# TensorE's queue in the order of the program, with the program's steps traced in another order

## The chip, the cores and the metric

The kernel runs on one core of one Trainium2 chip. The metric is the device time of one execution in microseconds (us). TensorE is called PE here, VectorE DVE, ScalarE ACT, GpSimd POOL and SyncE SP.

## What is computed

Two blocks in sequence on 256 tokens of width 1024, in float32. The first block (`first_block`, called b1 in the kernel) has two layers: banded attention with a sink and a dilated mixture, and latent attention with a rotary key. The second block has two layers on the same tokens (x) and on 256 context tokens (ctx). Each layer is a mixer and an expert feed-forward, `peer_ffn`:

```python
p = xn @ wl                        # q, k, v, pool, conv, gates: 10 x 1024 columns
o = blocked_diff_attn(q, k, v, lam)
mix = mixer_output(o, p, ...)      # gated sum of attention, pooling and convolution, then @ w_out
h = h + mod[:, 2] * mix
# peer_ffn: 8 heads, the best 16 of 16384 experts each
q = (xc @ w_q).reshape(chunk, 8, 2, 128)
s = einsum('thid,hikd->thik', q, sub_keys)        # two half keys, top 16 of each
# top 16 of the 256 sums, softmax -> gate, expert indices eidx
hid = gelu(einsum('td,thkd->thk', xc, u_emb[eidx]))
out = einsum('thk,thkd->td', gate * hid, v_emb[eidx])
```

The first layer's mixer runs on x and on ctx, the second's on x with only keys and values of ctx.

## The kernel before

**Work.** Activations lie transposed, channels on partitions, as eight chunks of 128 channels by 256 tokens. A weight chunk (128x1024 float32, 512 KB) makes 128 output channels of one product. Most chunks are split in two rounded halves `wa` (ACT, L281) and `wb` (DVE, L282), and multiply in 24 matmuls (L409 to L411, `mm3`). Chunks called whole skip the split and multiply as float32 (L416, `mm1`). `WS.get` loads three chunks ahead (two in the expert phase) and splits two ahead (one there).

**Experts.** `topk` makes the scores (L1241), picks the best 16 on DVE and transposes the choice (`id4`, L1344). `gbuild` turns the choice into a dense table of gates G (one-hot tables `hot` and `gat` on DVE, L1487 and L1489, matmuls L1495, ACT copies L1499, stores from the ACT queue L1504). `peer` then runs over all 128 expert rows: `hid(j)` multiplies chunk j of `pu` with x and applies gelu (L1528), `wgt(j)` multiplies with the gates `gp` (a load of G, L1548), `vside(j)` adds the product with chunk j of `pv` (L1570 to L1580). The first `npre` of the `hid` run before G is there, into buffers `gpre`; the first `nnat` of `pu` are whole. In layer 0 the experts of ctx are instead gathered row by row (`rows`: indirect loads from the POOL queue L1381, and on DVE L1392 and L1401), 512 row steps spread over other stages.

**Order.** The program is a set of Python generators that trace instructions; `par`, `lead`, `along` and `chain` decide by the numbers that are yielded (`yield 2.6`: a cost) which generator traces next. The context is opened with `schedule_with_timeline_sim=True`: a planner then sets each engine's queue by its own model of time. Of the instructions that are ready in that model it takes the one traced first, so that a later traced instruction comes ahead of one that waits there. On the chip each queue runs in the order so set. The planner also hands out the buffers: 42 of 4 KB a partition (tag `pg`, weight chunks and most activations), and PSUM banks, three of tag `u` for products and five of tag `m`.

**Stages.** b1 (`x`) runs beside the ctx mixer, its `choose` (the expert choice of ctx) and the modulation products (`mods`, L574): `lead(xs, (ctx..., 2.0))` gives ctx two units of cost for one of x. When ctx has come to its `rows`, x goes on alone with its own mixer (layer 0): `qkv`, then `attend` (`attn2`) and `branches` by `par` with rates 60 and 190. Then `ffn_start` (`topk`; then the rest of `topk`, `gbuild` and the early `hid` by `par`) and the loop of `peer`. Layer 1 follows in the same manner; there `kv_ctx` (the rest of the rows, the norm of ctx and its keys) and `attend` run beside `branches`.

**Norms.** `rms_bcast` squares on ACT (L472), sums on PE (L474, L479), makes the root on DVE (`rsqrt`, L403), a diagonal `dg` (L498), and spreads it with PE (L501). `norm_hl` and `norm_f` multiply and split. The head norm in `qkv` and the one after the attention have the same form (L946, L903, L905; L1046, L1056). The attentions run in three steps for each unit u: `first` (scores on PE, softmax on DVE and ACT), `second` (transposes, L656 and L1015), `third` (product with the values, L668 and L1026).

Of the kernel before, what the change touches and what calls it, by code (L numbers as in the profile page):

```python
# [34 lines left out]
NPRE = (16, 20), (20, 28)  # L35
# [257 lines left out]
class Ker:  # L293
# [170 lines left out]
    def rms_bcast(s, hch, n):  # L464

        nc = s.nc
        st = s.ps("m")
        if n == 8:

            for g in range(0, n, 4):  # L470
                sq = s.pg([128, 4, T], F32, "sq")
                nc.scalar.activation(sq, hch(g, 4), AF.Square)  # L472
                for k in range(4):
                    nc.tensor.matmul(st[32 * k:32 * k + 32, :T], s.ones[:, 0:32], sq[:, k], start=g == 0, stop=g == 4)  # L474
            gs = s.s1([128, T], "gs")
            nc.scalar.copy(gs, st[:, :T])
            ss = s.ps("m")
# [4 lines left out]
        else:  # L482
            for g in range(0, n, 4):
                m = min(4, n - g)
                sq = s.pg([128, 4, T], F32, "sq")
                nc.scalar.activation(sq[:, :m], hch(g, m), AF.Square)
                for k in range(m):
# [16 lines left out]
    def rms(s, h, n=8):  # L504
        rbs = s.s1([128, T], "rbs")
        s.nc.vector.tensor_copy(rbs, s.rms_bcast(lambda g, m: h.t[g // 4][:, :], n))
        return rbs

    def norm_hl(s, h, a, b, name, n=8, rbs=None):

        nc = s.nc
        rbs = rbs if rbs is not None else s.rms(h, n)
        o = HL(s, name, n)
        for k in range(n):
# [6 lines left out]
            else:  # L521
                nc.scalar.activation(oh, y, AF.Identity, bias=b(k))
                nc.vector.scalar_tensor_tensor(ol, y, b(k), oh, op0=OP.add, op1=OP.subtract)
        return o

    def norm_f(s, h, a, b, o):

        nc = s.nc
        rbs = s.rms(h)
        for k in range(8):  # L530
            y = s.s1([128, T], "ny")
            nc.vector.scalar_tensor_tensor(y, h.ch(k), a(k), rbs, op0=OP.mult, op1=OP.mult)
            nc.scalar.activation(o.ch(k), y, AF.Identity, bias=b(k))  # L533
        return o
# [88 lines left out]
    def attn_causal(s, scores, bias, init, scale, val, emit):  # L623
# [49 lines left out]
        for i in range(18):  # L673
            if i < 16:
                first(i)
            if 1 <= i < 17:
                second(i - 1)
            if i >= 2 and i % 2 == 1:
                third((i - 3) // 2)
            yield 1.7  # L680
# [12 lines left out]
    def b1(s, x, eng, out):  # L693
# [8 lines left out]
        hn = s.norm_hl(x, lambda k: s.V("norm_w", k), None, "hn")  # L702
        del x
        ws.load(W1)
        yield 1.0
# [81 lines left out]
        hn = s.norm_hl(x, lambda k: s.V("norm_w", 8 + k), None, "hn")  # L787
# [48 lines left out]
        cqn = s.norm_hl(cq, lambda k: s.V("cqn", k), None, "cqn", 2)  # L836
        ckn = s.norm_hl(ckv, lambda k: s.V("ckvn", k), None, "ckn", 1)
# [49 lines left out]
        rb = s.rms_bcast(lambda g, m: x.t[g // 4][:, :], 8)  # L887
# [7 lines left out]
    def rows_hl(s, rr, lo, n):  # L895
# [12 lines left out]
        nc.vector.tensor_tensor(rl[z], tb[z, :T], rh[z], op=OP.subtract)  # L908
        return rh[z], rl[z]


    def qkv(s, l, hn, ws, rope, want_q, r):
# [26 lines left out]
        for a, off, _ in todo:  # L939
            for hf in range(2):  # L940
                sq = s.pg([128, 4, T], F32, "sq")
                nc.scalar.activation(sq, a.t[hf], AF.Square)
                for k in range(4):
# [9 lines left out]
        rh, rl = s.rows_hl(rr, 0, 16)  # L953
        yield 8.0
# [29 lines left out]
    def attn2(s, l, q, kv, sr, o):  # L984
# [45 lines left out]
        for i in range(18):  # L1030
            if i < 16:
                first(i)
            if 1 <= i < 17:
                second(i - 1)
            if i >= 2:
                third(i - 2)
            yield 3.0

        bank = s.ps("m")
        for hf in range(2):  # L1040
            sq = s.pg([128, 4, T], F32, "sq")
            nc.scalar.activation(sq, o.t[hf], AF.Square)
            for k in range(4):
# [6 lines left out]
        rh, rl = s.rows_hl(rr, 64, 8)  # L1050
        yield 4.0
# [108 lines left out]
    def mixer(s, l, st, src, ws, eng, res, kvx, late=None, before=None, seq=False, h=None, rbs=None, side=None):  # L1160
# [7 lines left out]
        hn = s.norm_hl(h, lambda k: s.a1[l][:, k, st:st + 1], m0, "hn", rbs=rbs)  # L1168
# [50 lines left out]
        res["xn"] = s.norm_f(h, lambda k: s.a2[l][:, k, st:st + 1], s.mod(l, st, 3), Act(s, F32, "xn"))  # L1219
# [3 lines left out]
    def topk(s, l, xn, ws, eng, res, rows=False):  # L1223
# [8 lines left out]
        for h, sb in s.lin(ws, xn, 16):  # L1232
            if sb is None:
                yield 2.6
                continue
            qf = s.s2([128, 512], "qf")
            nc.scalar.copy(qf, sb)
# [17 lines left out]
            if h % 4 < 3:  # L1255
                continue
# [38 lines left out]
            for j in range(2):  # L1295
                for hf in range(2):
# [13 lines left out]
                    yield TY  # L1310
        ts = tp[:, 2].rearrange("p h t k -> p (h t) k")
# [158 lines left out]
    def gbuild(s, res, G, eng, ntc=8):  # L1470
# [7 lines left out]
        iob = io[:, None, :, :].to_broadcast(sh)  # L1478
        for tc in range(ntc):
            gt = [s.pg([128, 32, 32], F32, "gt") for _ in range(4)]  # L1480
            for q in range(4):
# [8 lines left out]
                for u in range(2):  # L1490
# [277 lines left out]
```

## Time and profile before

| | before |
|---|---|
| runs | 3692.51 to 3705.2 us, median of 3: 3701.63 us |
| profiled execution, own time | 3691.09 us |
| its span (first to last instruction) | 3689.3 us |
| PE busy | 3258.1 us, 88% |
| DVE busy | 2790.7 us, 76% |
| ACT busy | 1485.0 us, 40% |
| mean granted clock of PE | 0.932 of full |
| DMA | 941.10 MB, mean 255 GB/s |

Busy time is the union of an engine's instructions. A row with an idle time names what ended it. The granted clock has two levels, 1.2 and 2.4 GHz (0.5 and 1.0 in the rows); a mean between them says how the stretch divides.

### The profile page before, as it was taken

How to read it: one execution, taken by the hardware profiler on the slowest of the kernel's cores; microseconds unless marked ns; L12 is line 12 of the kernel's file. 1: busy time of each engine (PE TensorE's matmuls, PEld its weight loads, DVE VectorE, ACT ScalarE, POOL GpSimd, SP SyncE). 2: the span in 40 equal slices, each digit the busy share in tenths (PEclk: the TensorE clock that was granted, in tenths of full speed). 3: DMA queues.
4: the chain of work that ended last, by engine and by line, in shares of the span. 5: the costliest groups of instructions: out<-in, count | busy, mean ns of one | idle time of the engine just before them, and what ended most of it. 6: DMA issues, size and time to landing. Idle time of an engine off the chain costs nothing. (4 is left out here: it accounts for less than half of the span.)

```text
span 3689.3 us, 61049 instructions
## 1 busy us (share of the span) xinstructions
PE 3258.1 (88%) x23324; PEld 2966.9 (80%) x23324; DVE 2790.7 (76%) x5722; ACT 1485.0 (40%) x2785; POOL 935.6 (25%) x831
## 2 busy tenths in 40 slices
PE   6989989996799885679999999778998689999999
PEld 5976889766689774668888888767988589999999
DVE  4356585578899889799989999788465978777655
ACT  3444345323355313333443444333353154444443
POOL 2002101212343512365555555232000003111000
PEclk9989999998899897889999999888999899999999
DMA  8536446756688845999999999776525089888764
GB/s 298 160 126 215 146 138 189 274 183 225 238 299 280 321 161 181 344 408 386 384 379 386 379 387 381 248 280 231 158 88 192 12 262 354 307 285 286 263 217 153
DMA packets 315430, 941.10 MB, mean 255 GB/s; under 512 B 29616, under 2 KB 93136, under 8 KB 315136
## 3 DMA queue, kind: packets, MB, share of 16 engines
q1 hardware_dynamic: 130848, 468.77, 35.7%
q0 software_dynamic: 118816, 432.76, 32.3%
q10 hardware_dynamic: 65472, 35.66, 3.2%
q8 instruction: 183, 3.00, 0.3%
q14 instruction: 111, 0.91, 0.1%
HBM read 893.01 MB, written 43.02 MB: 254 GB/s over the span
## 5 line engine op out<-in xcount | busy, mean ns | idle before, releaser
L282 DVE TENSOR_TENSOR wb<-wr,wa 128x1024 fp32r<-128x1024 f32 x846 | 1015.4, 1222 | 321.5 <-ACT wa L281 304.9
L281 ACT CAST wa<-wr 128x1024 fp32r<-128x1024 f32 x846 | 856.3, 1046 | 108.3 <-DMA wr<-in_w 39.0
L409 PE MATMUL pu<-hnh,wa 128*128 128x256 f32 x2000 | 586.0, 293 | 47.9 <-ACT wa L281 45.9
L411 PE MATMUL pu<-hnh,wb 128*128 128x256 f32 x2000 | 583.4, 293 | 17.1 <-DVE wb L282 17.0
L410 PE MATMUL pu<-hnl,wa 128*128 128x256 f32 x2000 | 578.5, 290 | 0.0
L409 PE MATMUL pu<-xh,wa 128*128 128x256 f32 (+1 forms) x1760 | 492.1, 280 | 10.1 <-ACT wa L281 9.6
L1381 POOL DMA_INDIRECT row<-in_pu,ridx x256 | 365.1, 1426 | 520.7 <-DVE wb L282 124.5
L410 PE MATMUL pu<-xl,wa 128*128 128x256 f32 (+1 forms) x1760 | 491.2, 279 | 0.9 <-DVE xl L1538 0.9
L411 PE MATMUL pu<-xh,wb 128*128 128x256 f32 (+1 forms) x1760 | 491.4, 279 | 0.0
L1381 POOL DMA_INDIRECT row<-in_pv,ridx x256 | 354.4, 1384 | 473.5 <-DVE wb L282 133.0
L409 PEld LDWEIGHTS pu<-hnh,wa 128*128 128x128 f32 x2000 | 397.7, 199 | 65.0 <-ACT wa L281 52.0
L411 PEld LDWEIGHTS pu<-hnh,wb 128*128 128x128 f32 x2000 | 395.8, 198 | 32.5 <-DVE wb L282 21.9
L410 PEld LDWEIGHTS pu<-hnl,wa 128*128 128x128 f32 x2000 | 397.4, 199 | 3.9 <-issue 3.5
L409 PEld LDWEIGHTS pu<-xh,wa 128*128 128x128 f32 x1760 | 338.5, 192 | 20.1 <-ACT wa L281 14.5
L410 PEld LDWEIGHTS pu<-xl,wa 128*128 128x128 f32 x1760 | 338.5, 192 | 4.6 <-DVE xl L1538 1.1
L411 PEld LDWEIGHTS pu<-xh,wb 128*128 128x128 f32 x1760 | 338.5, 192 | 1.8 <-issue 0.4
L1401 DVE SCALAR_TENSOR_TENSOR racc<-row,rwg,racc 128x1024 f32<-128x1024 f32 x254 | 325.5, 1282 | 0.4
L416 PE MATMUL pu<-xn,wr 128*128 128x256 f32 (+1 forms) x1344 | 311.9, 389 | 4.7 <-ACT xn L533 4.7
L1392 DVE CUSTOM_DVE_ANT_0 row<-row,xr 128x1024 f32<-128x1024 f32 x256 | 311.2, 1221 | 0.0
L1528 ACT ACTIVATE gel<-pu 128x256 f32<-128x256 f32 (+1 forms) x208 | 77.2, 371 | 577.8 <-PE pu L411 553.0
L416 PEld LDWEIGHTS pu<-xn,wr 128*128 128x128 f32 x1344 | 261.6, 199 | 41.7 <-issue 6.2
L1570 PE MATMUL pm<-W,wa 128*128 128x224 f32 x1024 | 276.1, 275 | 1.6 <-ACT wa L281 1.6
(427 smaller groups left out, 6487.7 us busy)
## 6 DMA issues: line engine op xcount, KB each, us to landing
wr<-in_w SPq DMA_DIRECT2D x288, 512.0 KB
wr<-in_pu SPq DMA_DIRECT2D x256, 512.0 KB
wr<-in_pv SPq DMA_DIRECT2D x256, 512.0 KB
wr<-in_w POOLq DMA_DIRECT2D x130, 512.0 KB
wm<-in_wmod POOLq DMA_DIRECT2D x96, 512.0 KB
G<-gt ACTq DMA_DIRECT2D x60, 512.0 KB
gp<-G SPq DMA_DIRECT2D x32, 512.0 KB
gp<-G SPq DMA_DIRECT2D x32, 448.0 KB
```

The costliest lines, as they stand in the source:

```text
L281: nc.scalar.copy(a, r)
L282: nc.vector.tensor_tensor(b, r, a, op=OP.subtract)
L409: mm(out, ah, bh, start=i == 0, stop=False)
L410: mm(out, ah, bl, start=False, stop=False)
L411: mm(out, al, bh, start=False, stop=i == n - 1)
L416: s.nc.tensor.matmul(out, w[:, k * 128:(k + 1) * 128], x(k), start=k == 0, stop=k == 7)
L1381: nc.gpsimd.indirect_dma_start(out=t, out_offset=None, in_=tab[w], in_offset=bass.IndirectOffsetOnAxis(ap=s.ridx[:, tt, i:i + 1], axis=0))
L1392: v.tensor_tensor_reduce(t, t, xr[tt], 1.0, 0.0, OP.mult, OP.add, hid[:, i:i + 1])
L1401: v.scalar_tensor_tensor(out[tt], t, wg[:, i:i + 1], out[tt], op0=OP.mult, op1=OP.add)
L1528: nc.scalar.activation(g, bank[:, :NT], AF.Gelu_apprx_tanh)
L1570: mm(o, vh[:, c], W[:, 0], start=j == 0 and d % 2 == 0, stop=False, skip_group_check=True)
```

## The change

PE's queue is no longer the planner's: `manual_schedule` for PE makes it the order in which the program traces. The other engines and the buffers stay with the planner. With that the program traces in another order:

- `rms_bcast` yields between its steps, and with it `rms`, `norm_hl` and `norm_f`, which become generators; `rows_hl` and the head norms yield too. The context norm at the start is traced beside b1's.
- both attentions run `second` two steps behind `first` instead of one, `third` three or more behind, in 19 rounds instead of 18, of costs that keep the sum.
- `topk` traces the choice of a head (`select`) after the product of the next; `gbuild` traces the matmuls of a table (`tables`) after the one-hot tables of the next.
- `ffn_start` traces the early `hid` beside the tail of `topk` (`lead`, at 6 units for each unit of `topk` in layer 0, 4 in layer 1), and the rest beside `gbuild`, instead of all beside tail and `gbuild` by `par`.
- layer 0 takes `nnat, npre` = 20, 24 for 16, 20. Layer 1 keeps 20, 28.

```diff
-NPRE = (16, 20), (20, 28)
+NPRE = (20, 24), (20, 28)
+
+EARLY = (6.0, 50.0), (4.0, 65.0)
...
                 nc.scalar.activation(sq, hch(g, 4), AF.Square)
+                yield 1.5
                 for k in range(4):
                     nc.tensor.matmul(st[32 * k:32 * k + 32, :T], s.ones[:, 0:32], sq[:, k], start=g == 0, stop=g == 4)
             gs = s.s1([128, T], "gs")
             nc.scalar.copy(gs, st[:, :T])
+            yield 1.0
...
             nc.vector.tensor_scalar(dg[:, tt], s.C("ident"), r[:, tt:tt + 1], None, op0=OP.mult)
+        yield 4.0
         rb = s.ps("m")
...
-        for i in range(18):
+        for i in range(19):
             if i < 16:
                 first(i)
-            if 1 <= i < 17:
-                second(i - 1)
-            if i >= 2:
-                third(i - 2)
-            yield 3.0
+            if 2 <= i < 18:
+                second(i - 2)
+            if i >= 3:
+                third(i - 3)
+            yield 2.85
...
-        rh, rl = s.rows_hl(rr, 64, 8)
-        yield 4.0
+        yield 3.0
+        rh, rl = yield from s.rows_hl(rr, 64, 8)
...
+        prev = None
+        for h, sb in s.lin(ws, xn, 16):
+            if sb is None:
+                yield 2.6
+                continue
+            qf = s.s2([128, 512], "qf")
+            nc.scalar.copy(qf, sb)
+            if prev is not None:
+                yield from select(*prev)
+            prev = h, qf
+        yield 2.6
+        yield from select(*prev)
...
-        program(k, upto)
+
+        with tc.manual_schedule(engines={mybir.EngineType.PE}):
+            program(k, upto)
...
-def ffn_start(k, l, rx, ws, G, pe, tot, *more, ntc=8):
+def ffn_start(k, l, rx, ws, G, pe, early, tot, *more, ntc=8):
...
-    yield from par(k, (chain(tk, lambda: k.gbuild(rx, G, k.nc.scalar, ntc)), TG), (until(pe), tot), *more)
+    pre = until(pe)
+    yield from lead(tk, (pre, early))
+    yield from par(k, (k.gbuild(rx, G, k.nc.scalar, ntc), 64.0), (pre, tot), *more)
...
-    next(b1)
-    rbc = [k.rms(hc[0])]
     md = k.mods(0, gp)
+    rbc = []
+
+    def norm_ctx():
+        rbc.append((yield from k.rms(hc[0])))
+    drain(par(k, (until(b1), 1.0), (norm_ctx(), 1.0)))
     drain(until(md))
```

## Rows read from the trace of the kernel before

**Rows 1.** Page: busy us (share) of the engines; DVE's split, count, busy, mean ns.

```profile
PE 3258.1 (88%) x23324; PEld 2966.9 (80%) x23324; DVE 2790.7 (76%) x5722; ACT 1485.0 (40%) x2785; POOL 935.6 (25%) x831
...
L282 DVE TENSOR_TENSOR wb<-wr,wa 128x1024 fp32r<-128x1024 f32 x846 | 1015.4, 1222 | 321.5 <-ACT wa L281 304.9
```

**Rows 2.** Table by stretch; columns in its first line, x counts instructions.

```profile
core 0: us, PE busy (x) PEld busy (x) DVE busy (x) ACT busy (x) POOL busy (x), PEclk, DMA share, GB/s
190.00:300.00 110.00, 96.14 (x549) 78.37 (x549) 66.47 (x228) 49.97 (x149) 8.45 (x16) 0.78 0.37 120
440.00:540.00 100.00, 85.49 (x643) 82.72 (x643) 72.83 (x153) 39.06 (x58) 8.48 (x16) 0.90 0.37 120
840.00:1000.00 160.00, 117.95 (x753) 106.47 (x754) 128.13 (x261) 56.34 (x77) 47.14 (x37) 0.79 0.72 253
1000.00:1250.00 250.00, 234.43 (x1815) 221.50 (x1813) 233.70 (x399) 121.10 (x200) 102.56 (x73) 0.98 0.85 295
1370.00:1413.00 43.00, 2.06 (x9) 1.26 (x8) 40.96 (x227) 4.00 (x13) 0.94 (x1) 0.50 0.08 22
1413.00:1531.00 118.00, 91.75 (x719) 78.11 (x719) 109.30 (x167) 51.34 (x265) 35.38 (x26) 0.86 0.89 292
1700.00:2300.00 600.00, 556.78 (x3462) 499.85 (x3461) 549.25 (x725) 251.23 (x391) 328.92 (x223) 0.99 0.99 384
2350.00:2570.00 220.00, 176.03 (x1218) 165.53 (x1216) 180.75 (x285) 80.21 (x107) 64.64 (x55) 0.85 0.74 261
2914.00:2949.00 35.00, 5.67 (x27) 4.71 (x26) 33.26 (x184) 5.08 (x15) 0.00 (x0) 0.58 0.00 0
2949.00:3070.00 121.00, 109.25 (x984) 103.75 (x983) 83.81 (x127) 61.52 (x266) 7.46 (x7) 0.95 0.86 277
3100.00:3600.00 500.00, 500.00 (x4480) 500.00 (x4479) 358.71 (x471) 245.75 (x378) 65.97 (x51) 1.00 0.83 279
```

**Rows 3.** Timeline of PE, the norm of ctx in layer 1: start, us, instruction, [idle before].

```profile
2554.93 1.22 PE L501 MATMUL pm<-dg,ones 128*128 128x128 f32 x4 [2.74 <-DVE dg L498]
2563.03 0.58 PE L409 MATMUL pu<-hnch,wa 128*128 128x256 f32 x1 [6.87 <-ACT wa L281]
```

**Rows 4.** Timeline of PE, end of ctx's attention and start of b1's.

```profile
262.46 1.22 PE L757 MATMUL pm<-kava,q 64*128 64x256 f32 x2
...
266.17 0.87 PE L656 MATMUL pm<-ct,p 128*128 128x128 f32 x3 [2.07 <-DVE p L649]
266.84 6.82 PE L1046 MATMUL pm<-ones,sq 128*128 128x1 f32 x32
276.22 1.02 PE L903 MATMUL pm<-ct,rr 128*8 128x128 f32 x4 [2.56 <-DVE rr L403]
```

**Rows 5.** Timeline of PE, early `hid` chunk beside the table.

```profile
1434.38 3.67 PE L416 MATMUL pu<-xn,wr 128*128 128x256 f32 x16
```

**Rows 6.** Groups on DVE, 1413 to 1531: count | busy us, mean ns | idle before.

```profile
L1489 DVE TENSOR_TENSOR gat<-hot,id 128x1024 f16<-128x1024 f16 x64 | 41.4, 688 | 1.5
```

**Rows 7.** Waits of the SP queue from 1290 to 1560: us in total, times, longest.

```profile
SPq L268 <- DVE top L1309: 43.8, 1, 43.8
```

**Rows 8.** Timelines of ACT, SP and PE between the table and the expert loops.

```profile
1533.00 10.08 ACTq L1504 DMA_DIRECT2D G<-gt  x3
...
1543.29 0.33 SPq L1548 DMA_DIRECT2D gp<-G  x1
...
1560.91 1.71 PE L1578 MATMUL pm<-wa,W 128*128 128x512 f32 x4 [2.01 <-ACT wa L281]
...
3070.44 0.37 PE L1570 MATMUL pm<-W,wa 128*128 128x224 f32 x1 [1.38 <-ACT wa L281]
```

**Rows 9.** Timeline of PE, layer 0's attention norm: x16 squares, then a product.

```profile
1222.04 2.11 PE L1046 MATMUL pm<-ones,sq 128*128 128x1 f32 x16
1224.01 0.56 PE L409 MATMUL pu<-hnh,wa 128*128 128x256 f32 x1
```

**Rows 10.** Timeline of PE at the start.

```profile
52.27 0.58 PE L409 MATMUL pu<-hnh,wa 128*128 128x256 f32 x1 [6.08 <-ACT wa L281]
```

More of the change, by code (lines that the diff above doesn't have):

```diff
@@ L511, in norm_hl @@
         nc = s.nc
-        rbs = rbs if rbs is not None else s.rms(h, n)
+        if rbs is None:
+            rbs = yield from s.rms(h, n)
         o = HL(s, name, n)
@@ L528, in norm_f @@
         nc = s.nc
-        rbs = s.rms(h)
+        rbs = yield from s.rms(h)
         for k in range(8):
@@ L786, in b1 @@
         s.dump("x1", x)
-        hn = s.norm_hl(x, lambda k: s.V("norm_w", 8 + k), None, "hn")
+        hn = yield from s.norm_hl(x, lambda k: s.V("norm_w", 8 + k), None, "hn")
         yield 1.0
@@ L886, in b1 @@
         s.dump("x2", x)
-        rb = s.rms_bcast(lambda g, m: x.t[g // 4][:, :], 8)
+        rb = yield from s.rms_bcast(lambda g, m: x.t[g // 4][:, :], 8)
         for k in range(8):
@@ L1167, in mixer @@
         m0 = s.mod(l, st, 0)
[L1168 removed]
+        hn = yield from s.norm_hl(h, lambda k: s.a1[l][:, k, st:st + 1], m0, "hn", rbs=rbs)
         del h, rbs
@@ L1231, in topk, with select @@
         IX = s.sml([128, 8, 4, 16], "topi", H16, bufs=1)
[L1232 to L1237, printed above, removed]
+        def select(h, qf):
             sb = s.ps("m")
@@ L1478, in gbuild, with tables @@
         iob = io[:, None, :, :].to_broadcast(sh)
+        def tables(hot, gat, gt, tc, q):
+            for u in range(2):
+                bank = s.ps("m")
+                for i in range(4):
+                    t = u * 4 + i
+                    for j in range(2):
+                        mm(bank[:, i * 128:(i + 1) * 128], hot[:, 0, t // 2, :, t % 2], gat[:, j, t // 2, :, t % 2],
+                           start=j == 0, stop=j == 1)
+                for jq in range(4):
+                    o = q * 8 + u * 4
+                    nc.scalar.activation(gt[jq][:, :, o:o + 4],
+                                         bank.rearrange("p (t j) -> p j t", t=4)[:, jq * 32:(jq + 1) * 32, :],
+                                         AF.Copy, scale=1.0 / GS)
+                yield 1.0
+            if q < 3:
+                return
+            for jq in range(4):
+                eng.dma_start(G[jq * 8:(jq + 1) * 8, :, tc].rearrange("g p j t -> p g (j t)"),
+                              gt[jq].rearrange("p (g j) t -> p g (j t)", g=8))
+        prev = None
         for tc in range(ntc):
@@ L1489, in gbuild @@
                     v.tensor_tensor(gat[:, j], hot[:, 1], w[2 + j], op=OP.mult)
-                for u in range(2):
-                    bank = s.ps("m")
-                    for i in range(4):
-                        t = u * 4 + i
-                        for j in range(2):
-                            mm(bank[:, i * 128:(i + 1) * 128], hot[:, 0, t // 2, :, t % 2], gat[:, j, t // 2, :, t % 2],
-                               start=j == 0, stop=j == 1)
-                    for jq in range(4):
-                        o = q * 8 + u * 4
-                        nc.scalar.activation(gt[jq][:, :, o:o + 4],
-                                             bank.rearrange("p (t j) -> p j t", t=4)[:, jq * 32:(jq + 1) * 32, :],
-                                             AF.Copy, scale=1.0 / GS)
-                    yield 1.0
-            for jq in range(4):
-                eng.dma_start(G[jq * 8:(jq + 1) * 8, :, tc].rearrange("g p j t -> p g (j t)"),
-                              gt[jq].rearrange("p (g j) t -> p g (j t)", g=8))
+                if prev is not None:
+                    yield from tables(*prev)
+                prev = hot, gat, gt, tc, q
+        yield from tables(*prev)
     def peer(s, l, xn, G, eng, eng2, nnat, npre, out, keep=None, NT=T, rows=None):
```

44 lines of the change are left out of this document (26 added, 18 removed).

## The prediction

> **What bounds the kernel now.** I read the page first, then the table by stretch, then PE's timeline around its waits. PE is busy 88% of the span, more than any other engine [rows 1]. The table's clock column falls wherever PE is not dense [rows 2]. In it three kinds of stretch are to be told apart. From 3100 to 3600 PE is busy throughout at full clock: an order that only moves work can give nothing there. From 1700 to 2300 the DMA engines are busy 0.99 of the time, DVE 549 of 600 us and PE 557: three limits together. Everywhere else PE stands idle for some us at a time, waiting for a short chain on DVE and ACT, at half clock around it. These last are what the change is about.
>
> What such a stretch of length L loses I count as its idle time, plus half of that part of its low-clock time in which PE works. With mean clock m the low-clock time is 2(1-m)L, so the loss is idle + (2(1-m)L - idle)/2 where that is positive. By [rows 2], in us: 190 to 300 loses 13.9 + 17.2 = 31; 440 to 540 14.5 + 2.8 = 17; 840 to 1000 42 + 12.6 = 55; 1000 to 1250 16; 1370 to 1413 41; 1413 to 1531 26 + 3 = 30; 2350 to 2570 44 + 11 = 55; 2914 to 2949 29; 2949 to 3070 12. Of 286 us I have to say which part the new order reaches.
>
> The clock term is where the Trainium skill speaks against me. Its page "TensorE: Matmul & The Clock Gate", Part 1, says that for modelling the ramp costs under 1% of a typical span. By that rule all low clock here would cost under 37 us. The trace says otherwise: between 190 and 300 PE works 96 us at a mean clock of 0.78 [rows 2], and 17 us go there alone. The measurement decides; without the clock terms the sum below would be some 12 us smaller.
>
> **The change part by part.**
>
> *Norms with cover.* A norm is four PE steps with ACT and DVE between. With the yields, a product of the other generator now stands between them in PE's queue, where there is another generator: b1's second norm and its two small ones (ctx's `conv` to `co` chunks between, stretch 440 to 540), and ctx's norm in layer 1 (`branches` between). The first stretch loses 17; I take 13 (8 to 17, since the wait for the last split of the normed value remains). For the second the two waits are 2.74 and 6.87 us [rows 3]: 9.6, I take 10 with the clock around (0 to 20). No cover exists for the norm that ends b1, the first and second norm and the head norm of the x mixers: when they come, ctx is at its `rows` and no other generator traces PE work. So 840 to 1000, the largest loss, I set at 0 (-10 to 15). Norms: 23 (-2 to 52).
>
> *Attentions two steps apart.* Between 250 and 295 ctx's attention runs out of b1's products, which the planner had drawn ahead. Scores at 262.46, transposes of the unit before at 266.17 after 2.07 us idle, then the norm after the attention waits 2.56 more [rows 4]. In traced order b1's `z` chunks stay between the steps for two thirds of ctx's 16 units; after that its last units meet b1's own attention, as now. Of 31 I take half, 16 (0 to 25). In the x mixer of layer 0 each step has some 10 us of `branches` beside it either way; of 16 I take 8 (0 to 13). In layer 1 the attention's last units again outlast `branches`: 0. Attentions: 24 (0 to 38).
>
> *The start of the experts.* PE waits out the tail of `topk`: 41 us in layer 0, 29 in layer 1 [rows 2], for DVE. `lead` at 6 units a yield and 3.41 a chunk traces nine `hid` before the transposes of the choice; in layer 1, at 4 and 2.99, seven, and two just after. Nine chunks of 3.67 us [rows 5] are 33 us: they fit into 41. Each also issues its `pu` load on SP's queue; DMA share there is 0.08 in layer 0 and 0.00 in layer 1, so the loads cost nothing, if a buffer is free.
>
> What is late next? In layer 0 the table is DVE's: 64 `gat` of 688 ns [rows 6] and as many `hot`, 88 us, the rest of its 109 in 118 us [rows 2] being mostly row steps. It doesn't shrink when PE has less to do. After it ACT sits 10.08 us on the last stores of G, the first load of G issues at 1543.29, and `vside` starts at 1560.91 [rows 8]. That path remains, but nine 512 KB loads, 4.7 MB or 16 us at the 292 GB/s of this stretch, are no longer in its way. I take 10 (0 to 20). Four more `hid` before the loop take four loads out of it: 0.52 MB at 384 GB/s, 1.4 us each, 5 together. In exchange four chunks become whole and spare DVE's split. Layer 0: 15 (0 to 25).
>
> In layer 1 PE itself is the limit: busy 109 of 121 us [rows 2] until `vside` at 3070.44 [rows 8]. Nine chunks leave, 29 us. Then DVE's table (56 `hot`, 56 `gat`: 77 us from 2949) and the path through G are next: table until 3026, then the 28 us from the last stores to `vside` in layer 0 (1533.0 to 1560.9 [rows 8]) would allow 3054. So I take 16 (4 to 29). Start of the experts: 31 (4 to 54).
>
> *`topk` and `gbuild` a step later.* PE now has its next product ahead of the scores. The chain is DVE's in both; I take 0.
>
> *What the planner's order had hidden.* In front of traced order stands no later work. After layer 0's attention the squares at 1222.04 are followed at once by products of the gate after it [rows 9], which the program traces behind the whole norm. Without them PE waits for the evacuation of the last unit, the squares, the root and the spread: 2.56 us for the root where it stood open [rows 4], I take 7 in all, and the same in layer 1: -14 (-30 to -6). At the start b1's first products, now ahead of the modulation products, will queue behind these. PE stands idle 6.08 us before 52.27 for a later chunk's cast [rows 10], which covers most of that; -2 (-5 to 0). Sum -16 (-35 to -6).
>
> *Rows.* The new yields pace `rows` anew, on POOL's queue and DVE. In `ffn_start` the yields fall from 187 to 167, at 0.25 five row steps fewer; those that b1 and the x mixer gain (58 units, doubled for ctx, over 6.25) let some 15 more pass before. So ten fewer remain for layer 1. The steps move, none is added: 0.
>
> **Sum.** 23 + 24 + 31 - 16 = 62 us; all low ends -33, all high ends 138. The profiled execution took 3691.1 us; 62 less is 3629. The median of the runs shown lies 10.5 higher, and gives 3640. The middle of the ends, 52, lies close to the sum, but the places set at 0 hold the largest losses (840 to 1000), so I lean to the lower of the two and state 3632; the forecast's own range, some half of the way to the ends, is 40 us to either side: 3592 to 3672.
>
> **Rivals.**
>
> *Buffers hold the loads.* In layer 0 SP's `pu` load waited 43.8 us, to the end of DVE's choice, for a buffer [rows 7]. If early `hid` meet the same, nothing goes into the tail: 31 becomes 5, attentions reach half: 62 - 26 - 12 = 24, from the median 3677. For it: `tables` and `npre` 24 hold more buffers. Against: traced earlier, the loads come first when buffers are handed out, and each `hid` frees one.
>
> *More is reached than I count.* Half of what 840 to 1000 and the rest of 2350 to 2570 lose (55 + 45) and some of 1700 to 2300: 60 us on top of the forecast, 3572. By the Trainium skill's "Perfetto Trace Analysis", section Roofline, the 16 DMA engines give some 435 GB/s; then the loop of layer 0 would not be at its limit. Here the DMA engines are busy 0.99 at 384 GB/s [rows 2], so the measured limit is lower.
>
> *Slower: the queue stands at each attention step.* In traced order nothing passes a `second` whose softmax is late. From 190 to 300 PE works 96 us [rows 2] on some 22 units (ctx's 16, about six of b1) with the products between: 4.4 us a unit, 9 for two. The chain from scores to transposes took between 3.7 us, from 262.46 to 266.17 [rows 4], and twice that, the scores of that unit having come one unit earlier. It has six DVE operations; if each stands behind one split of 1222 ns [rows 1], 7.3 us are added to some 5, and each of 48 units (ctx, b1 twice) waits 3 us: 144 against the 62, 82 slower, 3784. It decides from 1.3 us a unit. Against it: DVE is busy only 66 of 110 us there.
>
> *No change.* The gaps close on PE, but DMA and DVE before and in the loop of layer 0 end when they ended: gain 0 to 10, 3695.
>
> **How the numbers follow.** The forecast 0.50; buffers 0.17; more 0.10; no change 0.08; slower 0.15. About 0.3%, 11 us, is what a measurement of this kernel can tell from no change. Faster by more: 0.50 + 0.17 + 0.10 = 0.77; within: 0.08; slower: 0.15. For 8 in 10 I leave out the slower case and the lower part of "more": 3560 to 3705.
>
> **What would show it.** Right: PE's 32 us before L1344 filled with L416; `vside` of layer 1 starting some 17 us sooner after the transposes; L501's waits gone in ctx's layer 1 norm; clock above 0.93. Wrong: L656 and L1015 waiting in many short pieces (slower case); SP's `pu` loads still late (buffers); 1700 to 2300 shorter (my limit wrong); new waits before L903 far over 7 us.

## The result, and the profile after

| | before | after |
|---|---|---|
| median of 4 runs each (lowest to highest) | 3697.18 us (3692.51 to 3705.2) | 3726.59 us (3724.61 to 3734.23) |
| ratio, 95% interval | | 1.0081 (1.0055 to 1.0107) |
| profiled span | 3689.3 us | 3722.8 us |
| mean granted clock of PE | 0.932 | 0.924 |

The kernel became 29 us slower, 22 beyond the upper end of the 8-in-10 range (3705); the forecast was some 60 faster. In the changed kernel L411 to L413 are the products (L409 to L411 before), L1508 the table's matmuls (L1495), L1610 to L1612 those of `vside` in layer 0 (L1578 to L1580), L283 and L284 the splits. The page's lines that answer to [rows 1]:

```profile
PE 3272.7 (88%) x23292; PEld 2981.4 (80%) x23292; DVE 2787.4 (75%) x5718; ACT 1480.3 (40%) x2779; POOL 904.7 (24%) x831
...
L284 DVE TENSOR_TENSOR wb<-wr,wa 128x1024 fp32r<-128x1024 f32 x842 | 1010.8, 1222 | 291.5 <-ACT wa L283 270.0
```

Nearly the same work takes PE 15 us longer. Where, the table by stretch says, cut at the same events as [rows 2] where those moved:

```profile
core 0: us, PE busy (x) PEld busy (x) DVE busy (x) ACT busy (x) POOL busy (x), PEclk, DMA share, GB/s
187.00:300.00 113.00, 104.00 (x664) 84.70 (x664) 78.19 (x289) 61.20 (x183) 12.10 (x23) 0.86 0.43 146
440.00:545.00 105.00, 101.42 (x839) 100.61 (x840) 81.63 (x134) 51.88 (x67) 14.46 (x28) 1.00 0.58 178
1188.00:1237.00 49.00, 35.66 (x244) 34.42 (x244) 37.65 (x59) 15.51 (x20) 12.51 (x9) 0.72 0.74 261
1533.00:2329.00 796.00, 708.97 (x4030) 618.98 (x4031) 700.55 (x929) 301.12 (x471) 392.97 (x292) 0.93 0.96 367
...
2971.00:3009.00 38.00, 37.64 (x323) 36.73 (x323) 37.17 (x61) 18.62 (x101) 0.00 (x0) 0.96 0.49 153
3009.00:3021.00 12.00, 11.84 (x101) 11.44 (x100) 0.61 (x2) 6.06 (x34) 0.00 (x0) 1.00 0.95 267
3021.00:3083.00 62.00, 43.23 (x408) 40.07 (x408) 43.00 (x59) 31.24 (x120) 4.80 (x5) 0.81 0.63 190
3083.00:3100.00 17.00, 3.55 (x61) 3.01 (x54) 2.29 (x7) 3.68 (x10) 0.93 (x1) 0.60 1.05 368
```

The first two lines are the places where the forecast wanted gains, and they came: from 440 to 545 PE now stands 3.6 us at full clock, where it stood 14.5 of 100 at 0.90. The third runs from the last product of layer 0's attention to the first `mh` product (the merged value times its weights), the fourth is the whole expert loop of layer 0, the last four the gate table of layer 1 and what follows it. The same stretches before:

```profile
1220.00:1251.00 31.00, 26.17 (x199) 25.03 (x198) 25.70 (x43) 11.96 (x16) 9.02 (x8) 0.94 0.93 340
1561.00:2319.00 758.00, 690.91 (x4104) 610.43 (x4105) 702.70 (x934) 306.62 (x479) 419.66 (x291) 0.97 0.99 386
...
2949.00:3035.00 86.00, 75.19 (x677) 71.52 (x677) 69.83 (x111) 44.87 (x234) 0.00 (x0) 0.93 0.83 253
3035.00:3070.00 35.00, 34.06 (x310) 32.23 (x308) 13.98 (x16) 16.65 (x34) 7.46 (x7) 1.00 0.94 335
```

Here is the span cut by events in PE's timeline (us; each row ends with the event; the last four columns are runs told of below):

| stage, up to | before | after | e1 | e9 | e5 | e16 |
|---|---|---|---|---|---|---|
| b1's outputs and ctx, to x's first scores | 981 | 948 | 949 | 951 | 959 | 960 |
| x mixer of layer 0 and norm, to the first keys | 327 | 341 | 338 | 341 | 326 | 327 |
| choice and table, to the first V | 253 | 243 | 250 | 247 | 252 | 250 |
| expert loop of layer 0, to the end of its last V | 758 | 797 | 751 | 751 | 754 | 752 |
| mixer of layer 1 and norm, to the first keys | 534 | 534 | 535 | 533 | 518 | 515 |
| choice and table, to the first V | 218 | 236 | 237 | 214 | 218 | 203 |
| expert loop of layer 1 | 611 | 615 | 615 | 615 | 612 | 611 |

After against before: 32 + 10 gained, 14 + 39 + 18 + 4 lost. The forecast's terms by the same cut: 29, 1, 10, 5, 3, 16, 0 gained, less 2 at the start. Two rows hide a loss behind the attention. From the attention's last product to the first `mh` product PE took 31 us before and 49 after in layer 0, 26 and 41 in layer 1. The mixer of layer 1 stays at 534 only because it gains some 15 us up to ctx's norm.

**The loop of layer 0.** PE's timeline of the changed kernel, as it returns about once in four steps:

```profile
1757.14 0.49 PE L1610 MATMUL pm<-wa,W 128*128 128x512 f32 x1 [1.71 <-ACT wa L283]
1758.40 0.50 PE L1611 MATMUL pm<-wb,W 128*128 128x512 f32 x1 [0.77 <-DVE wb L284]
1758.74 0.39 PE L1612 MATMUL pm<-wa,W 128*128 128x512 f32 x1
...
1759.28 0.63 PE L1611 MATMUL pm<-wb,W 128*128 128x512 f32 x1
1759.71 0.63 PE L1612 MATMUL pm<-wa,W 128*128 128x512 f32 x1
```

and of the kernel before, at the same point of its loop:

```profile
1756.87 1.20 PE L1578 MATMUL pm<-wa,W 128*128 128x512 f32 x4 [1.71 <-ACT wa L281]
1757.90 0.30 PE L409 MATMUL pu<-xh,wa 128*128 128x256 f32 x1
1758.04 0.28 PE L410 MATMUL pu<-xl,wa 128*128 128x256 f32 x1
1758.16 0.47 PE L1579 MATMUL pm<-wb,W 128*128 128x512 f32 x1
```

The wait of 1.71 us for `wa` is in both. Before, the planner had put the four L1578 of such a step first, though the program traces L1578, L1579, L1580 by turns, and two products behind them: `wb`, 1.2 us later, was there when it was needed. In traced order the second matmul needs `wb`: 0.77 us more, and from then the matmuls take 0.63 instead of 0.39 us; the clock has fallen, up to 1762.3. The next such wait ends at 1784.31, 27.17 us later; before, 24.56 (1756.87 to 1781.43).

**The table of layer 1.** `par` shares the tracing between table and early chunks by their weights, 64 and 65, and so one early chunk stands in PE's queue for every three table steps. From 2971 to 3009 PE and DVE are both full (37.64 and 37.17 of 38 us), and PE falls behind: its table steps start 0.1 us after DVE's `gat` at the beginning and 11.6 us after it at step 31. Then DVE, in its fixed queue, comes to a split whose `wa` ACT makes only behind copies and stores of table steps, and stands 12.06 us. By 3021 the eleven whole chunks beside the table are used up. The eight split ones, which before all come behind the table, now stand between its last 25 steps, and each asks ACT and DVE for its halves. PE works 43 of 62 us there at a clock of 0.81. The last step ends at 3082.6 instead of 3035.1. Of these 47 us, 21 are a later start and 26 the table itself, 6 in its first 31 steps and 20 in the others. Nothing is left then to cover the way through G (its stores, its first load, the first V). PE's timeline with some of its waits, the two longest of DVE (marked DVE), and the end of the table:

```profile
1205.53 0.81 PE L913 MATMUL pm<-ct,rr 128*8 128x128 f32 x3 [12.15 <-DVE rr L405]
...
2462.69 0.59 PE L915 MATMUL pm<-ct,rr 128*16 128x128 f32 x2 [18.20 <-DVE rr L405]
...
2561.29 0.58 PE L411 MATMUL pu<-hnch,wa 128*128 128x256 f32 x1 [4.60 <-ACT wa L283]
2564.49 0.58 PE L413 MATMUL pu<-hnch,wb 128*128 128x256 f32 x1 [2.41 <-DVE wb L284]
...
2968.68 1.29 DVE L1531 TENSOR_TENSOR hot<-io,id 128x1024 f16<-128x1024 f16 x2 [8.02 <-ACT io L1499]
...
3021.66 1.23 DVE L284 TENSOR_TENSOR wb<-wr,wa 128x1024 fp32r<-128x1024 f32 x1 [12.06 <-ACT wa L283]
...
3031.13 0.55 PE L411 MATMUL pu<-xh,wa 128*128 128x224 f32 x1 [4.68 <-ACT xh L1569]
...
3081.79 0.84 PE L1508 MATMUL pm<-gat,hot 128*128 128x128 f16 x6
3082.56 3.72 PE L1435 MATMUL pm<-ct,xn 128*32 128x128 f32 x64
3099.73 0.55 PE L1602 MATMUL pm<-W,wa 128*128 128x224 f32 x1 [13.45 <-ACT wa L283]
```

SP issues the first load of G at 3090.47, with the first of `pv` in its queue behind that; PE stands 13.45 us, where it worked 34.06 of 35 us before. Part of the later start is the wait of 8.02 us: ACT's queue has the gelu of two early chunks ahead of `io`. The first four lines are waits in norms, for later.

### The profile page after: what moved, and what is told of

It reads as the page before. It is cut to its first block, busy times and chain, and to the rows that moved or that the text cites. A ratio compares the mean times of both kernels' runs of the same rounds, so it can differ in the third digit from the quotient of the medians.

```text
span 3722.8 us, 60935 instructions
## 1 busy us (share of the span) xinstructions
PE 3272.7 (88%) x23292; PEld 2981.4 (80%) x23292; DVE 2787.4 (75%) x5718; ACT 1480.3 (40%) x2779; POOL 904.7 (24%) x831
## 5 line engine op out<-in xcount | busy, mean ns | idle before, releaser
L284 DVE TENSOR_TENSOR wb<-wr,wa 128x1024 fp32r<-128x1024 f32 x842 | 1010.8, 1222 | 291.5 <-ACT wa L283 270.0
L283 ACT CAST wa<-wr 128x1024 fp32r<-128x1024 f32 x842 | 850.6, 1046 | 81.7 <-issue 24.6
L411 PE MATMUL pu<-hnh,wa 128*128 128x256 f32 x2000 | 584.5, 292 | 15.3 <-ACT wa L283 15.0
L413 PE MATMUL pu<-hnh,wb 128*128 128x256 f32 x2000 | 579.6, 290 | 17.7 <-DVE wb L284 17.5
L411 PE MATMUL pu<-xh,wa 128*128 128x256 f32 (+1 forms) x1728 | 486.6, 282 | 10.2 <-ACT xh L1569 6.0
L413 PE MATMUL pu<-xh,wb 128*128 128x256 f32 (+1 forms) x1728 | 485.2, 281 | 1.3 <-DVE wb L284 1.3
L1404 POOL DMA_INDIRECT row<-in_pu,ridx x256 | 339.5, 1326 | 551.5 <-PE pu L413 119.8
L1404 POOL DMA_INDIRECT row<-in_pv,ridx x256 | 344.4, 1345 | 521.0 <-PE pu L413 161.7
L411 PEld LDWEIGHTS pu<-hnh,wa 128*128 128x128 f32 x2000 | 396.3, 198 | 26.2 <-ACT wa L283 16.2
L413 PEld LDWEIGHTS pu<-hnh,wb 128*128 128x128 f32 x2000 | 395.4, 198 | 21.9 <-DVE wb L284 21.6
L411 PEld LDWEIGHTS pu<-xh,wa 128*128 128x128 f32 x1728 | 336.3, 195 | 15.7 <-ACT xh L1569 6.5
L413 PEld LDWEIGHTS pu<-xh,wb 128*128 128x128 f32 x1728 | 335.1, 194 | 1.7 <-DVE wb L284 1.7
L418 PE MATMUL pu<-xn,wr 128*128 128x256 f32 (+1 forms) x1408 | 319.8, 386 | 3.2 <-ACT xn L542 3.2
L418 PEld LDWEIGHTS pu<-xn,wr 128*128 128x128 f32 x1408 | 273.4, 198 | 44.1 <-issue 10.0
```

What stands on the lines that cost most here:

```text
L283: nc.scalar.copy(a, r)
L284: nc.vector.tensor_tensor(b, r, a, op=OP.subtract)
L411: mm(out, ah, bh, start=i == 0, stop=False)
L413: mm(out, al, bh, start=False, stop=i == n - 1)
L418: s.nc.tensor.matmul(out, w[:, k * 128:(k + 1) * 128], x(k), start=k == 0, stop=k == 7)
L1404: nc.gpsimd.indirect_dma_start(out=t, out_offset=None, in_=tab[w], in_offset=bass.IndirectOffsetOnAxis(ap=s.ridx[:, tt, i:i + 1], axis=0))
```

## The experiments

All are compared with the kernel before by ratio. "After" is the changed kernel (1.0081). Differences between two runs are of their medians. The code cuts are shortened.

**e1, the order of the V step.** The changed kernel with one edit in `vside`:

```diff
-mm(bank, wh, vh[:, c], ...); mm(bank, wh, vl[:, c], ...); mm(bank, wl, vh[:, c], ...)   # bank by bank
+for a, b in ((0, vh), (1, vh), (0, vl)):
+    for tt in range(NT // 128):
+        w = W[:, a, tt * 128:(tt + 1) * 128]
+        for dh in range(2):
+            mm(acc[tt, dh], w, b[:, dh * 512:dh * 512 + 512], ...)
```

> The changed kernel, with one edit: in the expert loop of layer 0 the twelve V matmuls of a step stand in PE's queue as four on wa with the high part of W, four on wa with the low part, four on wb (in the changed kernel every second one of a bank needs wb). Theory A: the 38 us that this loop lost come from the order inside the V step. In the trace of the changed kernel PE waits 1.71 us for wa once in four steps, issues one matmul, waits 0.77 us for wb, and then runs 3.4 us at half clock; before, four matmuls that need no wb stood there, and no fall of the clock followed. So the period of four steps goes from 27.1 back to about 24.6 us, some 25 times: 55 to 62 us, time 3667 (3655 to 3685). Rival B: the loads of in_pv on SP, which in the changed kernel wait for PE to free a buffer (1768.2, 1774.0, 1782.4), set the period; then only the 0.77 us go, if at all: 3707 to 3727. Rival C: DMA and DVE limit the loop at a period longer than before: somewhere between, with DMA share at 0.99 or above.

3685.2 us, 0.9982 (0.9972 to 0.9992). The same matmuls in this run's timeline, and the loop in its table by stretch:

```profile
1728.00 2.11 PE L1610 MATMUL pm<-wa,W 128*128 128x512 f32 x8 [1.71 <-ACT wa L283]
1729.94 1.07 PE L1610 MATMUL pm<-wb,W 128*128 128x512 f32 x4
```

```profile
1537.00:2288.00 751.00, 676.18 (x4032) 601.12 (x4032) 696.21 (x928) 301.96 (x472) 418.02 (x292) 0.97 1.00 389
```

Theory A holds: the wait for `wb` is gone, the wait of 1.71 us alone leaves the clock up, and the loop takes 751 instead of 796 us. Of these 45 us, 12 are idle time (87.0 to 74.8), 33 the busy time of as many matmuls (708.97 to 676.18). By the clock's records the loop's time at the lower level falls from 107 to 45 us, and half of that difference is 31: the clock took nearly three times what the wait took. B, the loads that wait for PE, falls. I had expected 55 to 62 from a period of 27.1 us; on average it went from 26.5 to 24.9 only, since the changed kernel has shorter periods too, and e1 some of 26 to 27 us. What stretches those was not traced; the DMA share of 1.00 fits rival C as a rest.

**e2, the table first**, and **e9, both edits.**

```diff
-EARLY = (6.0, 50.0), (4.0, 65.0)
+EARLY = (6.0, 50.0), (4.0, 40.0)
```

> The changed kernel, with one number: the weight of the hid chunks beside the gate table of layer 1 from 65 to 40, so that about one chunk stands in PE's queue per five table steps and not per three. Theory A: in traced order the chunks between the table steps hold the table up (DVE busy 39.6 and 31.6 of 50 us there, 48.7 before), its last step moved from 3035 to 3082, and nothing was left behind it to cover the way through G: PE stood 13.45 us before the first V matmul. With fewer chunks between, the table ends near 3045, the rest of the chunks covers G's way, V starts near 3070 instead of 3100: time 3698 (3690 to 3710). Rival: the table is late because of buffers or of the loads of pu and not because of PE's queue; then V starts at 3090 or later and the time is 3717 to 3730.

> The changed kernel with both edits: V matmuls on wb last, and the weight of the chunks beside the table of layer 1 at 40. Theory: the two losses are independent; 3685 less the 21 us by which the start of the experts of layer 1 became shorter with the second edit alone (from the transposes of the choice to the first V matmul 120 instead of 141 us): 3664 (3655 to 3676). It stays behind the new tracing in the planner's order (3645), by what the two x mixers lose in traced order. Rival: the loop of layer 0 was ahead of its loads only because layer 1 came later, and the sum isn't reached: 3680 or more.

e2: 3713.9 us, 1.0046 (1.0028 to 1.0064); e9: 3662.5 us, 0.9921 (0.9904 to 0.9937). In e2 the last transposes of layer 1's choice and the first V are 121 us apart, 141 in the changed kernel. But choice and table of layer 0, of which nothing was changed, took 11 us longer there, and so e2 missed its 3698. The planner orders the other engines anew for every edit: DVE stands 13 us before splits in that table, 2 in the changed kernel. So some 10 us between two kernels can come from there. e9 came where the sum said. From e9, the table of layer 1 and what follows in the table by stretch, and the first V in PE's timeline:

```profile
2930.00:3015.00 85.00, 70.43 (x649) 65.51 (x648) 73.13 (x114) 46.11 (x233) 0.00 (x0) 0.92 0.77 236
3015.00:3038.00 23.00, 21.19 (x236) 20.64 (x233) 10.14 (x14) 12.28 (x29) 6.88 (x6) 1.00 0.96 358
```

```profile
3037.90 0.37 PE L1602 MATMUL pm<-W,wa 128*128 128x224 f32 x1 [1.81 <-ACT wa L283]
```

The table is DVE's again (73 of 85 us), and chunks cover G's way: 1.81 us of wait for 13.45. The traces agree on what goes with a long table of layer 1 (us, first to last matmul):

| | before | after | e1 | e5 | e2 | e9 | e16 |
|---|---|---|---|---|---|---|---|
| weight of the chunks | | 65 | 65 | 65 | 40 | 40 | 40 |
| split early chunks inside the table | 0 | 8 | 8 | all | 1 | 1 | 1 |
| table | 86 | 112 | 112 | 102 | 86 | 85 | 77 |
| its end to the first V | 35 | 17 | 17 | 17 | 22 | 23 | 25 |

The weight sets both PE's lag and which chunks come late; whole chunks throughout at weight 65 were not tried.

**e3, e4, e5: order and tracing apart.** e3 is the kernel before with the traced order alone, e5 the changed kernel without it, e4 with it only up to the loop of layer 0. The edit of e5:

```diff
-        with tc.manual_schedule(engines={mybir.EngineType.PE}):
-            program(k, upto)
+        program(k, upto)
```

> The kernel before, with only PE's queue in traced order; none of the new spacing, covers or early chunks. Theory: the two halves of the change belong together: without spacing PE stands at every second step of the attentions and at every norm, and the V order costs the same 55 to 60 us as in the changed kernel; 3830 (3780 to 3950). Rival: the spacing does little, the fixed queue is all that is seen: within 15 us of the changed kernel, 3712 to 3742.

> The changed kernel, with PE's queue in traced order only up to the expert loop of layer 0; from there on the planner orders PE as before (the new tracing stays throughout). Theory A: the 28 us that the changed kernel is ahead at the first V matmul are real and kept; the loop of layer 0 takes 745 to 760 us again, and the start of the experts of layer 1 is as before or up to 16 us earlier: 3655 (3640 to 3675). Rival B: what is gained ahead of the loop is given back in it, because DMA and DVE, not PE's order, set its end; it then ends at 2319 as before: 3690 to 3700.

> The changed kernel with the planner ordering PE everywhere, as before; only the new tracing (spacing, lags, early chunks) is left of the change. It is to be set beside the run in which traced order holds up to the loop of layer 0 (3645). Theory A: traced order earns something of its own in stage 1, since the planner draws b1's products ahead and leaves ctx's attention bare (190 to 300): ctx's rows start later than 785, the first V matmul of layer 0 comes at 1545 to 1560, time 3660 (3650 to 3685). Rival B: the spacing alone earns it and the planner is the better order everywhere: 3645 or less.

e3: 3818.6 us, 1.0336 (1.0319 to 1.0353). e4: 3645.4 us, 0.9871 (0.9855 to 0.9888). e5: 3645.1 us, 0.9864 (0.9846 to 0.9882). So the new tracing under the planner gains 47 us, and the queue in traced order takes 81 from it (3726.6 less 3645.1). Without the new tracing the same queue costs 126 us (e3). My theory for e5 fell: up to the loop of layer 0 traced order earns nothing. In the table above it is 8 us ahead at x's first scores (e9 against e5) and gives back more in the x mixer (341 against 327).

**e6, e7, e8 and e12, e14, e15: the parts undone**, in traced order and under the planner. Norms: the yields of `rms_bcast`, `norm_hl` and `norm_f` out; attentions: `second` one unit behind `first`; early: 0 for 6.0 and 4.0 in `EARLY`, weights 82 and 84.

> The changed kernel with the yields inside the norms taken out again (sums of squares, root, spread; the head norms keep theirs). The forecast put 13 us on b1's norms and 10 us on ctx's norm of layer 1. Theory A: these return as waits before the spread of the root and before the first product of a norm: stretch 440 to 540 loses some 19 us again (in the changed kernel it lost 3.6, before 22.9), the hnc norm 10: 3750 (3740 to 3765). Rival B: only the pace of the other generators moves and the waits land elsewhere: within 10 us of the changed kernel, 3716 to 3736.

> The changed kernel with the transposes of an attention unit one unit behind its scores again, not two, in both kinds of attention. Theory A: in traced order PE then stands at each second step for what of the softmax chain the products between don't cover; 16 units of ctx, 16 of b1 twice, and the x mixers with some 1 us each: 50 us slower than the changed kernel, 3775 (3750 to 3810). Rival B: the chain is covered with one unit as well, as the forecast's 24 us for all attentions say at most: 3727 to 3751.

> The changed kernel without hid chunks in the choice: all 24 and 28 of them stand beside the gate table (weights 82 and 84, so that they end with it). Theory A: PE waits the tail of the choice again, some 30 us in each layer; in layer 0 the table is DVE's and the chunks fit beside it, V starts 0 to 15 later than 1533; in layer 1 more chunks stand between table steps, V starts some 30 us later still: 3765 (3745 to 3785). Rival B: the tail is filled in vain in both layers, because DVE and G's way set V's start: 3722 to 3735.

> The new tracing in the planner's order (3645) with the attentions' transposes one unit behind the scores again. Theory A: the planner closes part of the gap that one unit leaves, and spacing is worth what the forecast gave all attentions, 24 us, not the 50 of traced order: 3668 (3658 to 3680). Rival B: with the planner the spacing of the attentions is worth nothing, the gain of the new tracing lies in norms and early chunks: 3640 to 3652.

> The new tracing in the planner's order (3645), with the yields inside the norms taken out. In traced order these were worth 31 us. Theory A: the planner puts cover between the steps of a norm by itself, so the yields are worth under a third of that: 3650 (3640 to 3657). Rival B: the planner doesn't see these waits, and the yields are worth as much as in traced order: 3670 to 3680.

> The new tracing in the planner's order (3645) without hid chunks in the choice (weights 82 and 84). In traced order they were worth 41 us. Theory A: the planner fills the tail of the choice with what is traced behind it only in part, as in the kernel before (32 and 21 us of waits there), and the early chunks are worth 10 to 25 us: 3662 (3655 to 3670). Rival B: PE is not what sets the start of V, and they are worth nothing: 3640 to 3650. Rival C: as in traced order, 3680 to 3690.

| undone | traced order | worth there | planner | worth there |
|---|---|---|---|---|
| norms | e6: 3757.9, 1.0179 (1.0161 to 1.0198) | 31 | e14: 3656.5, 0.9909 (0.9892 to 0.9927) | 11 |
| attentions | e7: 3776.3, 1.0219 (1.0200 to 1.0237) | 50 | e12: 3681.6, 0.9975 (0.9964 to 0.9986) | 37 |
| early chunks | e8: 3767.2, 1.0200 (1.0183 to 1.0217) | 41 | e15: 3679.6, 0.9975 (0.9961 to 0.9988) | 35 |

Each part's removal costs time in either order, more in traced order. e14's time lies at the upper end of its theory, that the planner covers norms by itself. But 11 us is a little over a third of the 31 (17 of 36 by the ratios) and no more than an edit elsewhere can move, so how much it covers stays open. e12 and e15 gave more than their theories, e15 nearly what it is worth in traced order. Under the planner the three sum to 83, more than the 47 of the whole tracing: they overlap, or the rest of it (the lags of `topk` and `gbuild`, 24 chunks for 20) costs something. That was not tried.

**e10, e11: cover for the norm after the attention.** The gate's products are traced beside the attention, their tanh kept in two `pg` buffers (e10 on e9, e11 on e5):

```diff
-yield from par(s, (attend(), 60.0), (s.branches(l, hn, ws, r), 190.0), *more)
+yield from par(s, (attend(), 60.0), (chain(s.branches(l, hn, ws, r), lambda: s.gate_th(ws, hn, ths)), 160.0), *more)
...
-yield from s.gate_add(ws, hn, o, mrg)
+s.gate_in(ths, o, mrg)
```

> As the run with both edits, and the products of the gate behind the attention are traced beside the attention (their tanh is kept until the attention's result is normed), so that in traced order there is PE work between the sums of the attention's squares and the step that needs the root. Theory: in the changed kernel PE stands 12.15 us there in layer 0 and 6.12 us in layer 1, since the gate's products stand behind the norm; with cover both waits fall under 2 us: 12 to 20 us better than the run with both edits, 3650 (3640 to 3660). Rival: what follows, the merged value and its splits, needs the norm all the same, and PE waits before the mh products instead: within 5 us of the run with both edits.

> The same early gate products with the planner ordering PE, and neither of the other two edits. Theory: the planner draws gate products into that wait by itself, so the edit gives nothing: 3645 (3638 to 3652). Rival: the tracing order also sets what ACT and DVE do first there, and the edit gives half of what it gives in traced order: 3630 to 3637.

e10: 3664.7 us, 0.9925 (0.9908 to 0.9942), no better than e9. e11: 3647.2 us, 0.9885 (0.9867 to 0.9904), as expected. PE's waits in e10, layer 0:

```profile
1222.50 0.81 PE L913 MATMUL pm<-ct,rr 128*8 128x128 f32 x3 [5.72 <-DVE rr L405]
...
1246.64 0.58 PE L411 MATMUL pu<-mhh,wa 128*128 128x256 f32 x1 [2.26 <-ACT mhh L462]
1248.32 0.58 PE L412 MATMUL pu<-mhl,wa 128*128 128x256 f32 x1 [1.10 <-DVE mhl L463]
```

The 12.15 us became 5.72, and new waits stand before `mh`, as the rival said. From the attention's end to the first `mh` product layer 0 takes 52 us (49 in e9). In layer 1 that stretch falls from 39 to 18, but the attention ends 10 us later. The mixers take 343 and 527 us for 341 and 533, and b1's stage 8 more, which I can't explain.

**e13, the mixer of layer 1 by the planner**, the rest as e9:

```diff
+    g.__exit__(None, None, None)        # the region of manual_schedule
     drain(k.mixer(1, 0, ...))
+    g = k.tc.manual_schedule(engines={mybir.EngineType.PE})
+    g.__enter__()
```

> Both edits (V matmuls on wb last, weight 40) with PE's queue in traced order everywhere but in the x mixer of layer 1, where the planner orders it. Theory A: with both edits 3662 is still 17 us behind the new tracing in the planner's order; by the milestones 17 to 23 us of that lie in this mixer (508 us from the last V matmul of layer 0 to the last mh product; 491 and 485 with the planner): 3643 (3635 to 3652). Rival B: what the planner wins there it gives back at the choice or the table of layer 1, which wait for DVE: 3655 to 3665.

3634.7 us, 0.9846 (0.9821 to 0.9870): 28 us better than e9, more than I had expected. That mixer in e9's table by stretch, cut at ctx's norm, and its longest wait in PE's timeline; then e13's table:

```profile
2291.00:2520.00 229.00, 169.81 (x1170) 157.29 (x1170) 181.56 (x319) 82.61 (x115) 62.67 (x47) 0.84 0.70 239
2520.00:2773.00 253.00, 239.27 (x1767) 223.41 (x1768) 154.57 (x279) 116.76 (x196) 6.33 (x12) 0.93 0.44 132
```

```profile
2422.78 0.59 PE L915 MATMUL pm<-ct,rr 128*16 128x128 f32 x2 [19.27 <-DVE rr L405]
```

```profile
2293.00:2514.00 221.00, 170.54 (x1183) 159.85 (x1182) 182.54 (x323) 84.94 (x118) 67.31 (x47) 0.85 0.72 248
2514.00:2748.00 234.00, 232.07 (x1745) 216.80 (x1745) 148.93 (x272) 112.83 (x192) 5.81 (x11) 0.97 0.44 138
```

19 of the 27 us lie behind ctx's norm: there PE stands 13.7 us in traced order and 1.9 under the planner, and works 239 us at 0.93 for 232 at 0.97. Of these, some 12 lie between the attention's last product and the first `mh` product (39 us in e9 with 6 idle, 27 in e13 with none), where the planner again fills the norm with the gate's products, and some 6 beside the attention. The wait of 19.27 us at the head norm is gone from e13's list of waits, but the stretch around it is only 8 us shorter.

**e16, the version the runs point to:** the new tracing under the planner (e5) with the two edits of e9.

> The new tracing in the planner's order (3645) with both edits (V matmuls on wb last, weight 40). Theory: the planner had already put matmuls without wb ahead, so the first edit gives 0 to 3 us; the second can give the 5 us by which the start of the experts of layer 1 was shorter in traced order with it (118 against 123): 3641 (3634 to 3648). Rival: fewer chunks beside the table change nothing under the planner, which draws table steps ahead anyway, or the other engines' order moves: 3645 to 3655.

3623.4 us, 0.9818 (0.9802 to 0.9835): the fastest, 66 us under before. Between the profiled executions of e5 and e16, 15 of 23 us lie between the choice of layer 1 and the first V (218 to 203): the share of chunks beside the table matters under the planner too, more than I had thought.

## Why the prediction was wrong, step by step

**"From 1700 to 2300 ... three limits together" was the step that failed first.** I read a stretch that is full as one that can't get better, and gave the loop only a gain of 5. It could get worse: 39 us. What hid `wb` there could be seen ahead. [rows 8] has "L1578 ... x4" where the program traces L1578, L1579, L1580 by turns: the planner had reordered inside the step. The part on what the planner's order had hidden looked at two norms and the start, 16 us in all; the largest such place was in the loop that runs 128 times. e1 shows it whole.

**"Then DVE's table ... and the path through G are next"** counted the chunks that move into the tail of `topk`, not where those that stay are put. The planner had run only whole chunks beside the table and kept the split ones for the time behind it. In traced order the weights 64 and 65 put all of them between its steps: PE fell behind, DVE stood before splits, and the table took 112 us for 86. Forecast 16 gained, measured 18 lost; e2 gives 20 back in that stretch, e9 22 against e1, with one number.

**Norms after the attention, 7 each.** The place was right and the size half of what came. From the attention's last product to the first keys layer 0 takes 101.5 us for 87.5, layer 1 90 for 76: 14 each, 28 for the 14 forecast, inside its 6 to 30. PE stood 12.15 us for the root in layer 0, where I took it from a wait of 2.56 us. The 14 are the whole loss of layer 0's mixer. e13 gives 12 back in layer 1, but e10's cover, the gate's products ahead of the norm, gave nothing back in layer 0; in the kernel before they stood inside it [rows 9].

**Norms, 23.** From 440 to 545 the loss is 3.6 us, from 17: 13 gained, as taken. The hnc norm waits 4.60 + 2.41 for the 9.61 of [rows 3]: 3 gained, not 10. 840 to 1000 stayed without cover, as said.

**Attentions, 24.** From 187 to 300 the loss by my measure is 9.0 + 11.3 = 20 for 31: 11 gained, not 16. In layer 0's x mixer the attention takes 240 us as before: 0 gained, not 8. The size of 24 was asked against the planner, where e12 says 37; so the term wasn't too large as a price of spacing, but in traced order not all of it came.

**The first stage came out right in part by luck.** It gained 32 us where 29 were forecast, but the two parts named make 24; the other 8 lie in places that I had not counted.

**Start in layer 0, 10.** The wait of 32 us before the transposes is gone, choice and table take 10 us less. As said, the table stays DVE's (112 of its 116 us, 109 of 118 before). What got shorter is the way from its end to the first V, 17 us for 30. That fits the loads that are out of the way, but no run takes them apart.

**Rows, 0.** Up to ctx's norm layer 1 gained some 15 us that no term has. 41 row loads were left there, 52 before, ten fewer as forecast; whether they are the cause was not tried.

**The slower rival** was the right outcome by the wrong mechanism. From 187 to 300 PE works 104 of 113 us: it doesn't stand at the attention steps, because they are two apart. With one (e7) it works 91 there, and the whole kernel is 50 us slower. What decided was the same property of a fixed queue, nothing passes a matmul that waits, at places that the change hadn't spaced.

**Clock.** I set the clock terms against a sentence of the Trainium skill's "TensorE: Matmul & The Clock Gate", Part 1 (a ramp under 1% of a typical span). I read it too widely: it stands with the slow matmuls at a kernel's start and does not speak of falls within a run. So it gives no bound of 37 us on all low clock, and my 17 us would not have broken that bound. What the trace shows is that the loop of layer 0 alone lost 33 us of busy time to falls of the clock, beside all other stretches.

**Open.** What in the mixer of layer 1 the planner puts where; whether split chunks or PE's lag cost the table of layer 1 more; why the splits came late in e2's layer 0.

## What to carry over

Before taking a queue from a planner, compare the order it made with the order of the program inside the hottest loop, one step of it, matmul by matmul: every difference there can be a wait that comes back as often as the loop does (here about once in four steps). Spacing work in the program and fixing the queue are two changes; the new tracing was good for 47 us, and the fixed queue cost 81. Where early work is woven into a chain that another engine paces, give it a share that leaves the chain its pace, keep for the time behind it the work that needs the pacing engine, and leave some work to cover that time.

## What was unexpected of the hardware

A single wait of 1.71 us in a full stream left PE at 2.4 GHz (e1: granted clock 1.00 from 1728.0 to 1730.9). From 1700 to 2300 e1 has 19 such waits and no fall of the clock after any; the kernel before has 19, with one fall. The same wait, one matmul, and a second wait of 0.77 us brought it to 1.2 GHz until 1762.3; from 1600 to 2300 there were 25 such pairs of waits and 21 falls of the clock (8 falls before). The loop paid 33 us of busy time for 12 of idle. And the DMA engines, at a share of 1.00, moved 389 GB/s in e1's loop, 386 at 0.99 before; the 435 GB/s that the Trainium skill's "Perfetto Trace Analysis", section Roofline, gives for them no loop here reached.
